# Stores of second-level block sums moved behind the loads on SyncE's queue, in the MLP of a one-core transformer layer

## The chip, the cores and the metric

The kernel runs on one core of a Trainium2 chip. The metric is device time in microseconds (us) of one execution, as the median of several runs. A profile of one execution says what each engine did and when: TensorE (PE, with weight loads as PEld), VectorE (DVE), ScalarE (ACT), GpSimd (POOL) and SyncE (SP, which here only issues transfers).

## The reference

One layer of a hybrid encoder on 1024 tokens of width 1024, in float32: two attention groups side by side, a cross-attention into 256 memory tokens, and a squared-ReLU MLP with hidden width 4096. Each is wrapped in root-mean-square norms and added to the residual. The change lies in the MLP alone:

```python
h = rmsnorm(x, g_ff_pre[l])
y = jnp.square(jax.nn.relu(h @ w_ff1[l])) @ w_ff2[l]
x = x + rmsnorm(y, g_ff_post[l])
```

## The kernel before

Every float32 operand of a product is split in a high and a low part, and a product is three matmuls (lines 193, 194, 195: high by high, low by high, high by low). The MLP's two matrix products are done by a seven-product block scheme: sums of blocks are multiplied instead of the blocks themselves, and the results are recombined.

The first half of the MLP is a loop over `j` = 0 to 15 (`NP` = 16), and the order of its instructions on each engine is the order in which the code is written. Iteration `j` works on two of the 32 row blocks of `w_ff1`, called blocks `j` and `j + 16`. What an iteration does, in this order:

- GpSimd makes the weight sums of iteration `j + 1` from its two raw blocks (`nxt.sums`, lines 2080 to 2082, and `nxt.sum4`, line 2087). They go into the tiles `sc` and `sd`.
- SyncE issues the load of the first raw block of iteration `j + 2` (`after.load(0)`, line 1833, tile `wf`).
- TensorE multiplies into the PSUM banks `px`, `pz`, `px` again (accumulating), `pv` and `pz` again (accumulating), 12 matmuls each. In the iterations below `AHEAD` = 7 the first row of products was done earlier and stored; it is loaded back a step ahead (`reload`, line 2102, tile `p1r`, two halves `p1` and `g11`). From `j` = 7 on it is multiplied in place.
- VectorE adds the products up. Line 2261 makes `u2` from the first `px` and `p1`; only after it may TensorE accumulate into that bank. Then `sums` of the iteration before (lines 2316, 2318, 2320 and 2322) is run, the low part of the next weights is made (`v0lo_s` or `v1lo_s`, line 1848), and lines 2277 and 2281 make `u3` and `g22` from the second `px` and from `pz`; only after line 2281 may TensorE accumulate into `pz`. Next come `wlo_s1a`, line 2299, the low part of `sd` (`u0lo_s` or `u1lo_s`) and line 2305.
- ScalarE makes the high parts of the weights and squares the clipped results (`relu2`, lines 1865 and 1866).
- SyncE stores the results: `put` (line 1869) into the buffers `gd`, and `put_parts` (lines 1885, 1887) into `gi1` and `gi5`. The loads of the second raw block of iteration `j + 2` (`after.load(1)`) and of `p1r` are issued in mid iteration, after line 2281.

Two of the seven results are taken through the block scheme a second time. For these the sums of two neighbouring iterations (an even and an odd `j`) are formed by `put_sums` in the even iteration that follows: four VectorE operations of 128x256 (lines 1893 to 1896) for form 1 in mid iteration, and four for form 5 at its end. `put_sums` returns a function that issues two stores (lines 1898 and 1899: `s12` and `s34` to `gi1S` or `gi5S`). These are the second-level forms:

```python
        return lambda: (
            nc.sync.dma_start(gi[n, ("S1", "S2")][s][:, :, k, :], s12.rearrange("p (a n) -> p a n", a=2)),
            nc.sync.dma_start(gi[n, ("S3", "S4")][s][:, :, k, :], s34.rearrange("p (a n) -> p a n", a=2)))
```

SyncE issues transfers strictly in the order written. It waits before each until its data are there or its target is free, and what stands behind waits with it. Raw blocks rotate through three buffers, and the tiles of results and sums through 18.

Of the kernel before, what the change touches and what calls it, by code (L numbers as in the profile page):

```python
# [135 lines left out]
def build(ctx, tc, nc, out, t):  # L136
# [13 lines left out]
    def mm_tile(shape, name, tag="mm"):  # L150
        return psp.tile(shape, F32, tag=tag, bufs=2, name=name)

    def u4(name, shape, dt=F32R):

        return up.tile(list(shape), dt, tag="u4", bufs=30, name=name)
# [1649 lines left out]
    def t2(name):  # L1805
        if region[0]:
            return pr.tile([P, HT], F32, tag="t2", bufs=9, name=name)
        return pf.tile([P, HT], F32, tag="t2", bufs=18, name=name)
# [3 lines left out]
    def bank(name, tag=None):  # L1812
        if tag is None:
            tag = ("mm", "s", "tr", "pv")[banks[0] % 4]
            banks[0] += 1
        return mm_tile([P, HT], name, tag)
# [47 lines left out]
    def relu2(c):  # L1864
        nc.scalar.activation(c, c, AF.Relu)
        nc.scalar.activation(c, c, AF.Square)
# [22 lines left out]
    def put_sums(n, j, c):  # L1889

        k, s, e = j // 2 % 4, j // 8, even.pop(n)
        s12, s34 = t2(f"s12_{n}{j}"), t2(f"s34_{n}{j}")
        nc.vector.tensor_add(s12[:, :HQ], e[:, HQ:], c[:, HQ:])
        nc.vector.tensor_sub(s12[:, HQ:], s12[:, :HQ], e[:, :HQ])
        nc.vector.tensor_sub(s34[:, :HQ], e[:, :HQ], e[:, HQ:])
        nc.vector.tensor_sub(s34[:, HQ:], c[:, :HQ], s12[:, HQ:])
# [3 lines that stand above are left out]
# [200 lines left out]
    def reload(j):  # L2100
        both = u4(f"p1r{j}", (P, 2, HT), F32)
        nc.sync.dma_start(both, p1d[j])
        saved[j] = both[:, 0, :], both[:, 1, :]
# [54 lines left out]
    def raw_b(q, k):  # L2158
        r = u4(f"wg{q}_{k}_{len(rows_b)}", (P, D), F32)
        nc.sync.dma_start(r, t["w_ff2"][q, k])  # L2160
        return r

    def fetch(s):

        n, k = steps[s]
        ra = wp.tile([P, D], F32, tag="wraw", bufs=3, name=f"ra{s}")
        rows_a[s] = ra
        if n in (("i", 0), ("i", 1)):
            name, h = inner[k // 2], k % 2
            nc.sync.dma_start(ra, gi[(1, 5)[n[1]], name][h].rearrange("p a b -> p (a b)"))  # L2170
            quads = {"A11": (0, 1), "A12": (2,), "S2": (3,), "S1": (), "S3": (0,), "S4": (3,), "A22": (2,)}[name]
            rows_b[s] = []
            for q in quads:
                rows_b[s].append(u4(f"wi{q}_{s}", (P, D), F32))
                nc.sync.dma_start(rows_b[s][-1], t["w_ff2q"][n[1], q, h])
            return
        i, name = order[n]
        nc.sync.dma_start(ra, gd[i][k].rearrange("p a b -> p (a b)"))
        if name == "T1":
            rows_b[s] = (raw_b(W12, k), raw_b(W11, k))  # L2180
        else:
            rows_b[s] = (raw_b({"B11": W11, "T2": W22, "T3": W11, "T4": W21}[name], k),)
# [50 lines left out]
        ops[s] = (ah, al, bh, bl)  # L2233

    with manual:
        sums = lambda: []
        for j in range(NP):
            more = j + 1 < NP
            after = Weights(j + 2) if j + 2 < NP else None
            w = cur.w  # L2240
            if more:
                nxt.sums()
                nxt.sum4()
            if after:
                after.load(0)
            elif more:
                fetch(0)
            if j < AHEAD:
                p1, g11 = saved.pop(j)
                x = bank(f"px{j}")  # L2250
            else:
                x, _, g11, add = first_row(j, w["a"])
                add()
            if not more:
                fetch(1)
                fetch(2)
                prepare(0)
            product(x, w["s23"], 0, XT["T2"], more=j >= AHEAD)
            u2 = t2(f"u2_{j}")
            if j < AHEAD:  # L2260
                nc.vector.tensor_add(u2, x, p1)
            else:
                nc.scalar.activation(u2, x, AF.Copy)
            forms = sums()
            relu2(g11)
            put(j, 0, g11)
            z = bank(f"pz{j}")
            product(z, w["s1a"], 0, XT["T1"])
            if more:
                if j + 1 >= AHEAD:  # L2270
                    nxt.split("a")
                if j:
                    nxt.split("s23")
            product(x, w["s23"], HT, XT["T3"], more=True)
            u3 = t2(f"u3_{j}")
            if j < AHEAD:
                nc.vector.tensor_add(u3, x, p1)
            else:
                nc.scalar.activation(u3, x, AF.Copy)
            g22 = t2(f"g22_{j}")  # L2280
            nc.vector.tensor_add(g22, z, u3)
            for form in forms[:1]:
                form()
            if more and not j:
                nxt.split("s23")
            if after:
                after.load(1)
            elif not more:
                prepare(1)
                fetch(3)  # L2290
            if j + 1 < AHEAD:
                reload(j + 1)
            v = bank(f"pv{j}")
            product(v, w["s1a"], HT, XT["T4"])
            if more:
                nxt.split("s1a")
            relu2(g22)
            put(j, 2, g22)
            nc.vector.tensor_sub(u3, u3, v)
            product(z, w["s4"], 0, XT["B22"], more=True)  # L2300
            if more:
                nxt.split("s4")
            relu2(u3)
            put_parts(1, j, u3)
            nc.vector.tensor_add(u2, z, u2)
            for form in forms[1:]:
                form()

            if not more:
                relu2(u2)  # L2310

            def sums(j=j, u2=u2, u3=u3, g11=g11, g22=g22):
                if j + 1 < NP:
                    relu2(u2)
                s1, s2, s4g = t2(f"s1_{j}"), t2(f"s2_{j}"), t2(f"s4_{j}")
                nc.vector.tensor_add(s1, u2, g22)
                put(j, 3, s1)
                nc.vector.tensor_sub(u2, g11, u2)
                put(j, 5, u2)
                nc.vector.tensor_sub(s2, s1, g11)  # L2320
                put(j, 4, s2)
                nc.vector.tensor_sub(s4g, u3, s2)
                put_parts(5, j, s4g)
                return [lambda: put_sums(1, j, u3)(), lambda: put_sums(5, j, s4g)()] if j % 2 else []

            cur, nxt = nxt, after
        prepare(2)
# [141 lines left out]
        for s, (n, k) in enumerate(steps[:-3]):  # L2469
            if s and s < len(steps) - 2:  # L2470
                prepare(s + 2)
            for read in reads:
                read()
            del reads[:]
            if s == 1:
                forms = sums()
            if s in (2, 3):
                forms.pop()()
            if s == 4:
                pfs.close()  # L2480
            if s + 4 == len(steps):
                prepare(s + 3)
            if s + 4 < len(steps):
                fetch(s + 4)
            if isinstance(n, tuple):
                inner_multiply(s)
                if k % 2:
                    reads.append(lambda x=n[1], p=k // 2: inner_read(x, p))
                for call in later[:1]:
                    call()  # L2490
                del later[:1]
                continue
            if k == 0:
                if n == 0:
                    X = four(f"fx{n}", ("mm", "s"))
                elif n == 3:
                    Y = four(f"fy{n}", ("tr", "pv"))
            banks = Y if n == 3 else X
            multiply(banks, range(4), [s], n in (2, 4, 6))
            for call in later[:1 if n < 6 else 2]:  # L2500
                call()
            del later[:1 if n < 6 else 2]
            if n == 6 and k in (3, 4):
                residual(2 * k - 2)
                residual(2 * k - 1)
            if k == NK - 1:
                for tp in range(4):
                    gather(n, tp, banks[tp])
                finished(n)
# [75 lines left out]
```

## Time and profile before

| | |
|---|---|
| median of 3 runs | 1463.97 us (1461.88 to 1464.31) |
| profiled execution | 1463.95 us, its span 1462.1 us |
| mean granted TensorE clock | 0.998 |
| TensorE busy | 1445.3 us, 99% of the span |
| VectorE, ScalarE, GpSimd busy | 1074.2, 844.6, 418.9 us |
| transferred | 255.29 MB, 175 GB/s in the mean |
| loop over `j`, iterations 2 to 5 | about 905 to 971 us of the span |

A row of a timeline holds the start, the duration, the engine, the line, the operation, and output and inputs by tile name (buffer numbers left out); in brackets stands how long the engine had been idle and what ended that. SPq rows are the issuing of a transfer, not the transfer. Matmuls overlap: the next starts before the one before it is shown as ended.

### The profile page before, as it was taken

The page shows a single profiled execution, that of the slowest core. Times are in us where ns is not written, and L with a number is a line of the kernel's source. Part 1 is how long each engine was busy: PE and PEld are TensorE (multiplying, and loading weights), DVE is VectorE, ACT ScalarE, POOL GpSimd, SP SyncE. Part 2 cuts the span into 40 slices and gives each one's busy share as a digit, 9 for nine tenths or more (in the row PEclk, how much of TensorE's full clock was granted, in tenths as well). Part 3 has the DMA queues.
Part 4 walks back from the last instruction along what each step waited for, and adds up shares of the span by engine and source line. Part 5 has one row for each costly group of instructions (what it writes and reads, how often), then busy time and mean ns, then how long its engine had stood idle before and what let it go on. Part 6 is the DMA issues. An engine that isn't in the chain of part 4 may idle for free.

```text
span 1462.1 us, 21876 instructions
## 1 busy us (share of the span) xinstructions
PE 1445.3 (99%) x7553; PEld 1232.0 (84%) x7553; DVE 1074.2 (73%) x1830; ACT 844.6 (58%) x1465; POOL 418.9 (29%) x520
## 2 busy tenths in 40 slices
PE   8999999999999999999999999999999999999998
PEld 8988888888889888888788888778888888888886
DVE  6777777767668847976873787785555776789897
ACT  6567677767677836555653455455555545555553
POOL 1245456545455301421321414333232000000003
PEclk9999999999999999999999999999999999999999
DMA  7132324321315595542531637775556897786885
GB/s 275 48 94 73 83 65 142 85 82 46 94 58 165 169 318 173 186 174 88 187 130 44 205 127 252 245 230 175 166 178 203 298 345 255 244 283 231 279 285 203
DMA packets 104351, 255.29 MB, mean 175 GB/s; under 512 B 11673, under 2 KB 30113, under 8 KB 104241
## 3 DMA queue, kind: packets, MB, share of 16 engines
q1 hardware_dynamic: 104096, 253.65, 52.6%
q8 instruction: 59, 0.97, 0.3%
q14 instruction: 52, 0.42, 0.1%
q10 hardware_dynamic: 144, 0.26, 0.1%
HBM read 184.07 MB, written 61.40 MB: 168 GB/s over the span
## 4 chain that ended last, share of the span: by engine, by line
PE 90%; DMA 3%; DVE 3%; issue 1%; ACT 1%; POOL 1%; SPq 0%; DVEq 0%; ACTq 0%
PE pv L754 4%; PE fx L194 4%; PE fx L193 4%; PE fx L195 4%; PE ptr L711 4%; PE px L194 3%; PE px L195 3%; PE px L193 3%; PE k L193 2%; PE q L193 2%; PE q L195 2%; PE q L194 2%; PE k L195 2%; PE k L194 2%; PE v L195 2%; PE v L193 2%
## 5 line engine op out<-in xcount | busy, mean ns | idle before, releaser
L717 DVE TENSOR_TENSOR phl<-ptr,phl 128x512 fp32r<-128x512 f32 (+1 forms) x152 | 92.5, 616 | 31.6 <-ACT phl L720 30.6
L720 ACT ACTIVATE phl<-ptr 128x512 fp32r<-128x512 f32 (+1 forms) x152 | 79.6, 539 | 40.3 <-PE ptr L711 38.5
L2357 POOL TENSOR_SCALAR rf<-sf 128x1 f32<-128x1 f32 x7 | 7.0, 1004 | 315.6 <-ACT jf L2338 315.4
L2229 ACT ACTIVATE whif<-ra 128x1024 fp32r<-128x1024 f32 x45 | 47.6, 1058 | 76.8 <-PE fx L194 34.7
L754 PE MATMUL pv<-phl,vs 128*128 128x512 f32 (+1 forms) x304 | 85.2, 366 | 0.2 <-DVE phl L717 0.2
L2231 DVE TENSOR_TENSOR wlof<-ra,whif 128x1024 fp32r<-128x1024 f32 x45 | 55.0, 1222 | 35.9 <-ACT whif L2229 35.8
L193 PE MATMUL fx<-vhif,whif 128*128 128x512 f32 x168 | 65.6, 391 | 0.0
L194 PE MATMUL fx<-vlof,whif 128*128 128x512 f32 x168 | 65.6, 391 | 0.0
L195 PE MATMUL fx<-vhif,wlof 128*128 128x512 f32 x168 | 65.4, 389 | 0.0
L754 PEld LDWEIGHTS pv<-phl,vs 128*128 128x128 f32 x304 | 55.2, 188 | 11.0 <-DVE phl L717 0.8
L2080 POOL TENSOR_TENSOR sc<-wf,wf 128x512 f32<-128x512 f32 x14 | 20.1, 1434 | 150.6 <-DMA wf<-in_w_ff 148.8
L768 POOL TENSOR_TENSOR o<-o 64x256 f32<-64x256 f32 x64 | 47.8, 747 | 52.7 <-DVE o L766 34.3
L766 DVE TENSOR_TENSOR o<-pv,o 64x512 f32<-64x512 f32 x64 | 44.0, 687 | 13.6 <-ACT o L771 12.2
L193 PE MATMUL k<-hT_hi,whik 128*128 128x512 f32 x128 | 53.6, 419 | 0.0
L193 PE MATMUL q<-hT_hi,whiq 128*128 128x512 f32 x128 | 51.6, 403 | 0.0
L193 PE MATMUL mq<-h2T_hi,whimq 128*128 128x512 f32 x128 | 51.4, 402 | 0.0
L195 PE MATMUL k<-hT_hi,wlok 128*128 128x512 f32 x128 | 50.4, 393 | 0.0
L193 PE MATMUL yw<-whiwo,yT_hi 128*128 128x512 f32 x128 | 50.3, 393 | 0.1
L195 PE MATMUL mq<-h2T_hi,wlomq 128*128 128x512 f32 x128 | 50.2, 392 | 0.2 <-DVE wlomq L455 0.2
L194 PE MATMUL k<-hT_lo,whik 128*128 128x512 f32 x128 | 50.3, 393 | 0.0
L195 PE MATMUL q<-hT_hi,wloq 128*128 128x512 f32 x128 | 50.2, 392 | 0.0
L194 PE MATMUL mq<-h2T_lo,whimq 128*128 128x512 f32 x128 | 50.2, 392 | 0.1
(715 smaller groups left out, 5214.6 us busy)
## 6 DMA issues: line engine op xcount, KB each, us to landing
wg<-in_w_ff SPq DMA_DIRECT2D x48, 512.0 KB, 6.2
ra<-gd SPq DMA_DIRECT2D x40, 512.0 KB, 4.4
wf<-in_w_ff SPq DMA_DIRECT2D x38, 512.0 KB, 4.5
wi<-in_w_ff2q SPq DMA_DIRECT2D x28, 512.0 KB, 5.5
wrawmq<-in_w_mq SPq DMA_DIRECT2D x16, 512.0 KB, 4.2
gd<-s SPq DMA_DIRECT2D x32, 256.0 KB, 2.1
gd<-g SPq DMA_DIRECT2D x25, 256.0 KB, 3.2
wrawq<-in_w_qk SPq DMA_DIRECT2D x8, 512.0 KB, 4.5
```

The costliest lines, as they stand in the source:

```text
L193: nc.tensor.matmul(ps, lh, rh, start=start, stop=False, skip_group_check=more)
L194: nc.tensor.matmul(ps, lh, rl, start=False, stop=False, skip_group_check=more)
L195: nc.tensor.matmul(ps, ll, rh, start=False, stop=stop, skip_group_check=more)
L711: nc.tensor.transpose(tr[:, m, :], sp[:, k * P:(k + 1) * P], ident)
L717: flow.put("V", at, 0.7, lambda: nc.vector.tensor_sub(pl[:, live, :], tr[:, live, :], f(ph[:, live, :])), done)
L720: flow.put("S", flow.end, 0.6, lambda ph=ph, tr=tr, live=live: nc.scalar.activation(ph[:, live, :], tr[:, live, :], AF.Copy), split)
L754: nc.tensor.matmul(pv[:, :, qs_, :], v, hl[:, :, hs, :], start=c == 0 and turn == 0, stop=last)
L766: flow.put("V", at, 0.7, lambda: nc.vector.tensor_add(o2[own], pv[own, :, :, ::step], o2[own]), lambda end: (free["pv"].give(end), flow.pu ...
L768: free["pv"].give(end), flow.put("G", end, 0.8, lambda: nc.gpsimd.tensor_add(o2[own, 0], o2[own, 0], o2[own, 1]), store)))
L2080: eng.tensor_sub(sc[:, k1], r0[:, k0], r1[:, k0])
L2229: nc.scalar.activation(ah, ra, AF.Copy)
L2231: nc.vector.tensor_sub(al, ra, f(ah))
```

## The change

The stores of a second-level form are no longer issued by the code that computes its sums. `put_sums` is called at the same place as before, so the four additions stay where they are, but the function that it returns is kept in a list `stores` and called later: for form 1 after the load of the second raw block and of `p1r`, for form 5 after the load of the first raw block at the head of the next iteration. In the second half of the MLP, where the last pair's forms are made, the two steps are still done at once.

```diff
-        sums = lambda: []
+        sums, stores = (lambda: []), []
         for j in range(NP):
...
             if after:
                 after.load(0)
             elif more:
                 fetch(0)
+            for store in stores:
+                store()
             if j < AHEAD:
                 p1, g11 = saved.pop(j)
                 x = bank(f"px{j}")
...
             nc.vector.tensor_add(g22, z, u3)
-            for form in forms[:1]:
-                form()
+            stores = [form() for form in forms[:1]]
             if more and not j:
                 nxt.split("s23")
             if after:
                 after.load(1)
...
             if j + 1 < AHEAD:
                 reload(j + 1)
+            for store in stores:
+                store()
             v = bank(f"pv{j}")
             product(v, w["s1a"], HT, XT["T4"])
...
             nc.vector.tensor_add(u2, z, u2)
-            for form in forms[1:]:
-                form()
+            stores = [form() for form in forms[1:]]
...
-                return [lambda: put_sums(1, j, u3)(), lambda: put_sums(5, j, s4g)()] if j % 2 else []
+                return [lambda: put_sums(1, j, u3), lambda: put_sums(5, j, s4g)] if j % 2 else []
...
-                forms.pop()()
+                forms.pop()()()
```

On TensorE, VectorE, ScalarE and GpSimd the order of instructions is the same before and after. On SyncE, iteration `j` = 2 and the head of `j` = 3 read as follows (the first `wf` with its `p1r` is for `j` = 4 and 3, the second `wf`, behind `gi1A`, for `j` = 5; `s_11` and `s_51` are the sums of forms 1 and 5):

```order
 L1869 DMA gd_1_9277<-p1r_10155 128x512
+L1833 DMA wf_10276<-in_w_ff 128x1024
+L2102 DMA p1r_10278<-p1d_9335 128x1024
 L1898 DMA gi1S_9346<-s_11_10270 256x1x256
 L1899 DMA gi1S_9348<-s_11_10271 256x1x256
-L1833 DMA wf_10278<-in_w_ff 128x1024
-L2102 DMA p1r_10280<-p1d_9335 128x1024
 L1869 DMA gd_1_9293<-g_2_10268 128x512
 L1885 DMA gi1A_9342<-u_2_10266 128x256
+L1833 DMA wf_10335<-in_w_ff 128x1024
 L1898 DMA gi5S_9354<-s_51_10323 256x1x256
 L1899 DMA gi5S_9356<-s_51_10324 256x1x256
-L1833 DMA wf_10337<-in_w_ff 128x1024
```

Two loads moved ahead of form 1's pair of stores and one ahead of form 5's; the stores keep their order among themselves. The same happens around `j` = 4 and 5.

From `j` = 7 on there is no `p1r` to load back. On SyncE, iteration `j` = 8 and the head of `j` = 9 (the first `wf` is for `j` = 10, the second for `j` = 11):

```order
+L1833 DMA wf_11092<-in_w_ff 128x1024
 L1898 DMA gi1S_9346<-s_17_11086 256x1x256
 L1899 DMA gi1S_9348<-s_17_11087 256x1x256
-L1833 DMA wf_11094<-in_w_ff 128x1024
 L1869 DMA gd_4_9296<-g_8_11084 128x512
 L1885 DMA gi1A_9343<-u_8_11082 128x256
+L1833 DMA wf_11149<-in_w_ff 128x1024
 L1898 DMA gi5S_9354<-s_57_11137 256x1x256
 L1899 DMA gi5S_9356<-s_57_11138 256x1x256
-L1833 DMA wf_11151<-in_w_ff 128x1024
```

One load moved ahead of each pair of stores. The even iterations 6, 10 and 12 read alike; at `j` = 14 there is no load left to pass, and nothing moved.

## The prediction

> **What bounds the kernel now.** The share of busy time by engine comes first, then the stages around the edit, then who keeps TensorE waiting there.
>
> ```profile
> PE 1445.3 (99%) x7553; PEld 1232.0 (84%) x7553; DVE 1074.2 (73%) x1830; ACT 844.6 (58%) x1465; POOL 418.9 (29%) x520
> 885.00:980.00 95.00, 90.64 (x390) 73.66 (x389) 69.90 (x94) 46.49 (x68) 39.21 (x28) 0.98 0.72 244
> 980.00:1140.00 160.00, 160.00 (x707) 132.27 (x706) 95.23 (x143) 84.00 (x126) 43.73 (x32) 1.00 0.55 179
> 1140.00:1200.00 60.00, 60.00 (x266) 49.59 (x265) 44.14 (x50) 30.10 (x38) 0.00 (x0) 1.00 0.93 335
> PE pz L193 <- DVE g L2281: 4.0, 2, 2.2
> ```
>
> In the stage rows the columns after the length are busy PE, PEld, DVE, ACT, POOL, then granted clock and DMA share. TensorE is full nearly everywhere, so only its holes can be won. The edit acts in iterations j = 2 to 13, and of that stretch only 885 to 980 us has holes: 4.4 us idle, plus a clock of 0.98. The last row names the holes: two waits of the product L193 for the addition L2281 on VectorE. The two later stage rows are full (160.00 of 160.00, 60.00 of 60.00), so what is won ahead of them is not taken back by a wait that exists today.
>
> The matmuls show both places, j = 3 and j = 5.
>
> ```profile
> 925.90 0.39 PE L193 MATMUL pz<-T_hi,whi_s1a 128*128 128x512 f32 x1
> 928.39 0.39 PE L195 MATMUL pz<-T_hi,wlo_s1a 128*128 128x512 f32 x1
> 936.70 0.47 PE L193 MATMUL pz<-B_hi,u1hi_s 128*128 128x512 f32 x1 [2.19 <-DVE g L2281]
> 940.65 0.39 PE L194 MATMUL pz<-B_lo,u1hi_s 128*128 128x512 f32 x1
> 941.10 0.39 PE L193 MATMUL px<-T_hi,v0hi_s 128*128 128x512 f32 x1
> 936.70:940.80 4.10, 4.10 (x11) 3.25 (x12) 2.27 (x3) 2.85 (x5) 1.22 (x1) 0.58 0.85 300
> 957.42 0.39 PE L193 MATMUL pz<-T_hi,whi_s1a 128*128 128x512 f32 x1
> 968.26 0.47 PE L193 MATMUL pz<-B_hi,u1hi_s 128*128 128x512 f32 x1 [1.85 <-DVE g L2281]
> 968.57 0.40 PE L194 MATMUL pz<-B_lo,u1hi_s 128*128 128x512 f32 x1
> ```
>
> From 925.90 to 928.39 there are 11 steps, 0.2265 us each. From the first product pz of an iteration to the next iteration's px stand 48 matmuls, 48 x 0.2265 = 10.87 us without a hole. In j = 3 it took 941.10 - 925.90 = 15.20, an excess of 4.33. Of that 1.68 is no wait: after the 2.19 us hole the clock is 0.58, and ten matmuls take 940.65 - 936.70 = 3.95 instead of 2.27. In j = 5 the same stretch ends at 968.57 + 11 x 0.2265 = 971.06, so it took 13.64, an excess of 2.77; the clock held. **The most that can be won is 4.33 + 2.77 = 7.1 us.**
>
> Why L2281 is late: the chain that ended last, the store queue, and the engines it feeds.
>
> ```profile
> 922.09 3.46 DMA p1r<-p1d
> 926.14 5.44 DMA wf<-in_w_ff
> 916.87 0.56 SPq L1869 DMA_DIRECT2D gd<-p1r  x1
> 920.18 0.52 SPq L1898 DMA_DIRECT2D gi1S<-s  x1
> 921.46 0.58 SPq L1833 DMA_DIRECT2D wf<-in_w_ff  x1
> 922.09 0.44 SPq L2102 DMA_DIRECT2D p1r<-p1d  x1
> 912.32 1.29 POOL L2087 TENSOR_TENSOR sd<-wf,sc 128x512 f32<-128x512 f32 x1
> 926.75 1.29 POOL L2080 TENSOR_TENSOR sc<-wf,wf 128x512 f32<-128x512 f32 x1 [13.14 <-DMA wf<-in_w_ff]
> 928.12 1.29 POOL L2081 TENSOR_TENSOR wf<-wf 128x512 f32<-128x512 f32 x1
> 931.18 1.63 POOL L2087 TENSOR_TENSOR sd<-wf,sc 128x512 f32<-128x512 f32 x1
> 927.93 0.63 ACT L1865 ACTIVATE p1r<-p1r 128x512 f32<-128x512 f32 x1 [2.54 <-DMA p1r<-p1d]
> 922.47 0.69 DVE L1848 TENSOR_TENSOR u1lo_s<-sd,u1hi_s 128x512 fp32r<-128x512 f32 x1
> 923.99 0.42 DVE L1893 TENSOR_TENSOR s<-s,s 128x256 f32<-128x256 f32 x1
> 927.99 0.69 DVE L2261 TENSOR_TENSOR u<-px,p1r 128x512 f32<-128x512 f32 x1 [2.46 <-issue]
> 928.60 1.36 DVE L2316 TENSOR_TENSOR s<-u,g 128x512 f32<-128x512 f32 x1
> 931.58 1.78 DVE L2320 TENSOR_TENSOR s<-s,p1r 128x512 f32<-128x512 f32 x1
> 934.01 1.22 DVE L1848 TENSOR_TENSOR v0lo_s<-sc,v0hi_s 128x1024 fp32r<-128x1024 f32 x1
> 935.86 0.69 DVE L2281 TENSOR_TENSOR g<-pz,u 128x512 f32<-128x512 f32 x1
> ```
>
> SyncE waits from 917.43 to 920.18 for the forms' sums, and the loads `wf` and `p1r` stand behind that store. `p1r` lands at 927.9; only then can L2261 run (its product px had ended when pz began, 925.90). From 927.99 VectorE is busy without a gap until L2281 ends at 936.55: a chain of 8.56 us, where TensorE has 36 matmuls, 8.16 us, and reaches that point at 934.3. The chain is that long because GpSimd's weight sums, released by `wf`, run at the same time: L2316 and L2320 take 1.36 and 1.78 where such an operation takes 0.69 (u1lo_s, same size).
>
> **The change part by part.**
>
> *The loads.* No computing instruction is added, dropped or moved; in j = 2, 4, ... 12 the mid-iteration loads pass form 1's two stores, and the load at the next head passes form 5's two. The buffer of `wf` in j = 2 was last read by GpSimd's L2087, 912.32 + 1.29 = 913.61, so the load can be issued when the store before it is, at 917.43 + 0.1 = 917.5, and `p1r` at 918.1. Both are 4.0 us earlier. At the next head, `wf` for j = 5 moves from 926.14 to about 924.3; nobody waits for it yet.
>
> *The stores.* They still wait for the same sums, so gi1S goes out at 920.2 as before. The forms' stores are read only in the second half of the MLP, and their tiles are two of 18 buffers; a delay under 1 us is free. Queued behind them is only what was behind them before. This costs 0.
>
> *`p1r` in j = 3.* Issued 4.0 earlier it lands at about 923.9, before px ends. L2261 is no longer held by it, and could start at 926.1: 1.9 us of the chain are gone.
>
> *`wf` in j = 3, and the contention that moves with it.* From issue to GpSimd's start:
>
> ```profile
> 952.98 0.57 SPq L1833 DMA_DIRECT2D wf<-in_w_ff  x1
> 958.32 1.28 POOL L2080 TENSOR_TENSOR sc<-wf,wf 128x512 f32<-128x512 f32 x1 [13.35 <-DMA wf<-in_w_ff]
> 966.59 0.40 SPq L1833 DMA_DIRECT2D wf<-in_w_ff  x1
> 970.55 1.30 POOL L2080 TENSOR_TENSOR sc<-wf,wf 128x512 f32<-128x512 f32 x1 [6.17 <-DMA wf<-in_w_ff]
> ```
>
> 5.3 us (here and in j = 2) and 4.0 us at the quickest: GpSimd starts between 921.5 and 922.8; I take 922.5, 5.0 after the issue. Its four operations then lie over VectorE's u1lo_s and the four operations of the second form (from 923.99) instead of over L2316 to L2320. How that goes the rows show: GpSimd's L2081 ends at 928.12 + 1.29 = 929.41, and L2316, begun within it, ends at 929.96, 0.55 later; L2087 ends at 932.81, L2320 at 933.36, again 0.55. An operation that reads SBUF twice does its work only after GpSimd's current one; L2261, with one operand in PSUM, took its 0.69 under GpSimd. The form's operations are 128x256 (0.42 against 0.69, a row not seen under GpSimd here), so their bounds are 0.42, unhindered, and a full hand-over, 0.42 - 0.69 + 0.55 = 0.28 after each end of GpSimd, whose next operation ends about 1.15 later (929.96 to 931.10, the start of L2087 at 931.18 less 0.08).
>
> The Trainium skill, "SBUF — State Buffer", section "SBUF: two separate sides", calls this an exclusive lock between GpSimd and a VectorE operation with two SBUF inputs: whichever starts first holds the pair for the whole instruction. It speaks against the change, since it predicts the full hand-over for the form's operations too; by it alone the sum below would be 1458.9, by free running 1456.9. The trace agrees with it for 128x512.
>
> With the full hand-over and a start at 922.5: u1lo_s ends 923.16, GpSimd's first 924.3; first form operation 924.6, GpSimd 925.75; second 926.05, 927.2; third 927.5, 928.65; fourth 928.95; then L2261 until 929.6. TensorE's second product px, which accumulates on the bank that L2261 reads, is due at 928.62 and starts about 1.0 late. From there GpSimd is done: L2316 to the end of L2281 take 4 x 0.66 + 1.22 + 2 x 0.7 = 5.3, ending at 934.9, and TensorE needs it 24 matmuls, 5.44 us, after px starts, at 935.1. So there is no second hole, and a hole of 1.0 us is well below 1.85, after which the clock held. With a start at 921.5 one form operation less collides, L2261 ends at 929.0 and the hole is 0.4. I take 0.9 per iteration, near the slower end since two of three intervals were 5.3.
>
> *j = 5* is the same, with `wf` issued up to 0.6 later for the reason next: 0.9 as well.
>
> *j = 4 and 6, unchanged code, but later against TensorE.* VectorE's chain now stands nearer behind TensorE, so the loads issued after L2322 do too.
>
> ```profile
> 935.02 0.40 SPq L1833 DMA_DIRECT2D wf<-in_w_ff  x1
> 939.58 1.28 POOL L2080 TENSOR_TENSOR sc<-wf,wf 128x512 f32<-128x512 f32 x1 [6.76 <-DMA wf<-in_w_ff]
> ```
>
> Today GpSimd starts 1.5 us before px of j = 4 (941.10). After: L2322, the last ahead of v0lo_s, ends about 932.3 instead of 934.0; the load follows it by 1.0 as today, at 933.3; GpSimd starts 4.56 later as today, at 937.9; and px of j = 4 is at 941.10 - (4.33 - 0.9) = 937.7. GpSimd starts with px instead of 1.5 before it, and two of VectorE's sums collide with it, at about 1.0 each (1.78 - 0.69 and less). Unhindered the chain is 0.7 for L2261 and the 5.3 from above, with the collisions 8.0, and 8.16 is allowed. I count 0.
>
> *j = 7 to 13.* `p1r` is gone there. The sums collide with forms as above, up to 4 us of VectorE, and what hides it is VectorE's idle time behind the forms:
>
> ```profile
> 1028.67 0.69 DVE L1910 TENSOR_TENSOR g<-py,p 128x512 f32<-128x512 f32 x1 [2.86 <-issue]
> 1033.15 0.69 DVE L2316 TENSOR_TENSOR s<-u,g 128x512 f32<-128x512 f32 x1 [3.78 <-ACT u L1866]
> ```
>
> 2.86 + 3.78 us per iteration; without that cover it would be a hole of about 1 us in each of four. I count 0, neither gain nor loss.
>
> *The sum.* 7.1 - 2 x 0.9 = 5.3 us. The profiled execution took 1463.95 us (span 1462.1 and 1.85 around it), the median of the runs is 1463.97, so the two agree: 1463.95 - 5.3 = **1458.7 us**. One run took 1461.88, 2.1 less, which a run without the stretch of slow clock (1.68) would nearly explain.
>
> The Trainium skill, "TensorE: Matmul & The Clock Gate", section "Part 1: The HAM clock gate", says that the clock halves after an idle window of about 3.4 us that runs freely; the trace partly agrees: 2.19 us sufficed once, 1.85 did not. By that page the 1.68 is a matter of where the window fell, and 5.3 would be 3.6 in an execution that had no slow stretch.
>
> **The rivals.** Differences under 0.2%, 2.9 us, are within what a measurement of this kernel can tell from none.
>
> *The hole moves to L2261* (0.12). If `wf` lands later than I take, 6.5 us after its issue since stores and `p1r` share the engines, GpSimd starts at 924.0, the four form operations all collide, L2261 ends at 930.65, px is 2.0 late, and the second hole is about the old one less 0.6. For it: DMA is busy 0.72 in this stage. Against it: no interval here was over 5.4. Gain 2 x 0.6, with the slow clock kept: 1462.8.
>
> *Slower: the collision passes to j = 4 and 6* (0.08). If GpSimd starts over 1.5 us after px there, its sums cover L2316 to L2320 as they do today in j = 3 (926.75 against px's end at 925.90), and TensorE waits there instead, each time with the slow clock: 2 x 4.33 = 8.7 lost, 5.3 won, 1467.3. Against it: the load would have to slip by another 1.5 us.
>
> *The change does nothing* (0.08): the loads are issued earlier but land as late, because the DMA engines are full with the stores issued up to 916.87. Then 1463.95. Against it: transfers issued 3 us later land within 5.3.
>
> **How the numbers follow.** The forecast, 0.72: 1456.9 (no hole left) to 1460.5 (holes of 1.8). The range reaches up into the first rival, to 1462.0, leaving out about half of that one and the two others, some 0.2. Faster than 1461.0: the forecast, 0.72, and a quarter of the first rival, 0.75. Slower than 1466.9: 0.08. Within: 0.17.
>
> **What would show it.** Right: in j = 2 and 4 `wf` and `p1r` issued 2.5 us or more ahead of gi1S; the row of L193 waiting for L2281 gone or under 0.5 in total; a wait of px for L2261 of 0.4 to 1.0, twice; the clock 1.00 from 885 to 980; form 5's operations L1893 to L1896 stretched at the end of even j. Wrong: those four at 0.42 with GpSimd's sums beside them; a wait for L2281 in j = 4 or 6; `wf` still landing 9 us after 917.5; new holes after 980 us.

## The result, and the profile after

The changed kernel takes 1458.65 us (median of 5 runs) against 1463.97 us for the kernel before (5 runs beside it). The ratio is 0.9966, with a 95% interval of 0.9952 to 0.9979. The medians differ by 5.3 us, which is the gain that was forecast; by the interval it lies between 3.1 and 7.0 us. The profiled execution took 1457.34 us, its span 1455.5.

The profile of the changed kernel: busy time by engine, the same stages as in the prediction (length, then busy PE, PEld, DVE, ACT, POOL, granted clock, DMA share), and all waits of TensorE from 890 to 1200 us.

```profile
PE 1443.5 (99%) x7553; PEld 1231.0 (85%) x7553; DVE 1089.6 (75%) x1830; ACT 844.4 (58%) x1465; POOL 423.3 (29%) x520
885.00:980.00 95.00, 93.61 (x411) 76.57 (x410) 77.42 (x101) 50.22 (x74) 41.78 (x30) 1.00 0.77 256
980.00:1140.00 160.00, 160.00 (x708) 132.48 (x707) 105.60 (x137) 83.42 (x125) 44.24 (x31) 1.00 0.54 179
PE px L193 <- DVE u L2263: 1.3, 2, 0.8
```

The two waits of pz for g (4.0 us) are gone. In their place stand two waits of px for u, 1.3 us together. The clock of the stage is 1.00 where it was 0.98, and the stage behind is as full as before. VectorE is busy for 15 us more (1089.6 against 1074.2) and the kernel is faster all the same: an operation that stands still beside GpSimd counts as busy (u1lo_s below is shown with 1.52 us, 0.69 before).

The timeline of the changed kernel in j = 2 and 3, by engine: SyncE's issues, GpSimd's weight sums, VectorE, TensorE. Lines behind the edit have moved by a few numbers; L2263 and L2283 are what L2261 and L2281 were.

```profile
916.10 0.40 SPq L1833 DMA_DIRECT2D wf<-in_w_ff  x1
916.55 0.44 SPq L2102 DMA_DIRECT2D p1r<-p1d  x1
918.73 0.52 SPq L1898 DMA_DIRECT2D gi1S<-s  x1
922.90 0.37 SPq L1833 DMA_DIRECT2D wf<-in_w_ff  x1
925.44 0.53 SPq L1898 DMA_DIRECT2D gi5S<-s  x1
920.70 1.29 POOL L2080 TENSOR_TENSOR sc<-wf,wf 128x512 f32<-128x512 f32 x1 [8.51 <-DMA wf<-in_w_ff]
922.07 1.62 POOL L2081 TENSOR_TENSOR wf<-wf 128x512 f32<-128x512 f32 x1
923.77 1.36 POOL L2082 TENSOR_TENSOR sc<-wf,wf 128x512 f32<-128x512 f32 x1
925.21 1.36 POOL L2087 TENSOR_TENSOR sd<-wf,sc 128x512 f32<-128x512 f32 x1
935.94 1.30 POOL L2080 TENSOR_TENSOR sc<-wf,wf 128x512 f32<-128x512 f32 x1 [9.37 <-DMA wf<-in_w_ff]
921.02 1.52 DVE L1848 TENSOR_TENSOR u1lo_s<-sd,u1hi_s 128x512 fp32r<-128x512 f32 x1
923.06 0.91 DVE L1893 TENSOR_TENSOR s<-s,s 128x256 f32<-128x256 f32 x1
924.01 1.40 DVE L1894 TENSOR_TENSOR s<-s,s 128x256 f32<-128x256 f32 x1
925.34 1.52 DVE L1895 TENSOR_TENSOR s<-s 128x256 f32<-128x256 f32 x1
926.78 0.41 DVE L1896 TENSOR_TENSOR s<-s,s 128x256 f32<-128x256 f32 x1
927.12 0.68 DVE L2263 TENSOR_TENSOR u<-px,p1r 128x512 f32<-128x512 f32 x1
924.46 0.39 PE L193 MATMUL pz<-T_hi,whi_s1a 128*128 128x512 f32 x1
927.85 0.50 PE L193 MATMUL px<-T_hi,v1hi_s 128*128 128x512 f32 x1 [0.51 <-DVE u L2263]
936.14 0.39 PE L193 MATMUL px<-T_hi,v0hi_s 128*128 128x512 f32 x1
956.18 0.50 PE L193 MATMUL px<-T_hi,v1hi_s 128*128 128x512 f32 x1 [0.84 <-DVE u L2263]
```

The loads now go out 2.6 us ahead of form 1's first store (916.10 against 918.73), where they followed it. GpSimd is done at 926.57, so the chain from u to g behind it runs without collisions. The profiled execution gained more than the medians, 6.6 us: pz of j = 3 begins at 924.46 instead of 925.90, 1.44 us earlier, ahead of anything that the edit touches. The remaining 5.1 to 5.2 us are won behind it.

For all comparisons below I use one measure. The **excess** of an iteration is the time from its first px to the first px of the next one, less its 60 matmuls at 0.2266 us each. It holds waits and slow clock together. In the changed kernel j = 3 has 0.80 us and j = 5 has 1.14.

### The profile page after: what moved, and what is told of

Read it like the earlier page. It is cut to its first block, busy times and chain, and to the rows that moved or that the text cites. A ratio compares the mean times of both kernels' runs of the same rounds, so it can differ in the third digit from the quotient of the medians.

```text
span 1455.5 us, 21885 instructions
## 1 busy us (share of the span) xinstructions
PE 1443.5 (99%) x7553; PEld 1231.0 (85%) x7553; DVE 1089.6 (75%) x1830; ACT 844.4 (58%) x1465; POOL 423.3 (29%) x520
## 4 chain that ended last, share of the span: by engine, by line
PE 94%; DVE 3%; issue 1%; ACT 1%; DMA 0%; SPq 0%; DVEq 0%; ACTq 0%
PE pv L754 4%; PE fx L193 4%; PE fx L194 4%; PE fx L195 4%; PE ptr L711 4%; PE px L193 3%; PE px L194 3%; PE px L195 3%; PE k L193 2%; PE yw L193 2%; PE mq L195 2%; PE q L193 2%; PE q L194 2%; PE q L195 2%; PE k L194 2%; PE mq L194 2%
## 5 line engine op out<-in xcount | busy, mean ns | idle before, releaser
L194 PE MATMUL q<-hT_lo,whiq 128*128 128x512 f32 x128 | 50.2, 392 | 0.0
```

Of the source, the lines that this page charges most:

```text
L194: nc.tensor.matmul(ps, lh, rl, start=False, stop=False, skip_group_check=more)
```

## The experiments

The theory, as in the prediction: the loads of `wf` and `p1r` behind form 1's stores make the hole; both are won by passing these stores; what is left is the hand-over between GpSimd's sums and VectorE's; form 5's part of the edit is worth nothing. The rivals: form 5's part matters; one of the loads would have been enough; the rest has another cause.

The runs in one table. The gain is one minus the ratio, times 1463; the excess is that of the profiled execution, in us. The experiments were run in groups, each beside its own runs of the kernel before (medians of 1463.34, 1462.99 and 1462.77 us), so kernels of different groups are compared by their ratios. The edits of the experiments are against the changed kernel, unless another is named.

| kernel | ratio to before, 95% interval | gain, us | j=3 | j=4 | j=5 | j=6 | sum |
|---|---|---|---|---|---|---|---|
| before | | | 4.32 | 0 | 2.77 | 0.23 | 7.3 |
| the change | 0.9966 [0.9952, 0.9979] | 5.0 | 0.80 | 0 | 1.14 | 0.30 | 2.2 |
| only form 1 passed | 0.9988 [0.9979, 0.9998] | 1.8 | 1.02 | 0.45 | 1.90 | 5.50 | 9.3 with 0.4 in j=7 |
| only form 5 passed | 0.9999 [0.9990, 1.0007] | 0.1 | 3.04 | 0 | 3.14 | 1.26 | 7.4 |
| only `p1r` ahead | 0.9977 [0.9967, 0.9986] | 3.4 | 1.55 | 0 | 1.87 | 0.25 | 3.7 |
| only `wf` ahead | 0.9987 [0.9978, 0.9996] | 1.9 | 0.49 | 1.25 | 1.68 | 2.56 | 6.0 |
| `p1r` ahead, form 5 passed | 0.9977 [0.9969, 0.9986] | 3.4 | 1.56 | 0 | 1.95 | 0.19 | 3.7 |
| loads behind g22's store | 1.0000 [0.9991, 1.0010] | 0 | 3.0 | 0 | 3.3 | 0.19 | 6.5 |
| form 5's sums later | 0.9965 [0.9952, 0.9977] | 5.1 | 0 | 0 | 0 | 0.27 | 0.3 |

The ratio stands for all executions of a kernel, the excess for the profiled one alone, and they need not agree. With only form 1 passed the profiled execution took 1464.01 us, 2.2 more than the median of that kernel, so its excess of 9.3 us, more than before the change, is larger than in a usual execution. With only `wf` ahead it took 1463.04 us against a median of 1462.36.

**Only form 1's stores are passed.** Form 5's pair goes out as before the change, ahead of the next head's load:

```
             nc.vector.tensor_add(u2, z, u2)
-            stores = [form() for form in forms[1:]]
+            for form in forms[1:]:
+                form()()
+            stores = []
```

> Only the stores of form 1 are moved (mid-iteration loads ahead of them); those of form 5 stay ahead of the load at the next head. Theory (the mid-iteration loads of p1r and wf are what was late): the whole gain, 1458.7 us, within 0.7 of the change; no wait of L193 for L2281; waits of px for L2261 of 1.3 us in all as in the change. Rival (the load at the head matters too): part of the gain is missing, 1460.5 or more, and a wait that the change does not show.

It took 1461.79 us against 1463.34, about a third of the gain. My expectation failed and the rival was right. Waits of TensorE, then SyncE, ScalarE, GpSimd and TensorE in the timeline, then two stretches in the stage view, all of this kernel:

```profile
PE pz L193 <- DVE g L2283: 3.0, 2, 2.8
PE px L193 <- DVE u L2263: 2.3, 2, 1.6
925.46 0.52 SPq L1898 DMA_DIRECT2D gi5S<-s  x1
927.80 0.60 SPq L1833 DMA_DIRECT2D wf<-in_w_ff  x1
961.51 0.40 SPq L1833 DMA_DIRECT2D wf<-in_w_ff  x1
961.96 0.52 SPq L2102 DMA_DIRECT2D p1r<-p1d  x1
969.56 0.63 ACT L1865 ACTIVATE p1r<-p1r 128x512 f32<-128x512 f32 x1 [1.63 <-DMA p1r<-p1d]
968.47 1.29 POOL L2080 TENSOR_TENSOR sc<-wf,wf 128x512 f32<-128x512 f32 x1 [11.99 <-DMA wf<-in_w_ff]
979.55 0.76 PE L193 MATMUL pz<-B_hi,u0hi_s 128*128 128x512 f32 x1 [2.81 <-DVE g L2283]
961.00:969.00 8.00, 8.00 (x37) 6.64 (x36) 4.55 (x7) 4.23 (x7) 0.53 (x1) 1.00 1.03 364
979.00:983.00 4.00, 3.44 (x8) 2.80 (x9) 3.97 (x8) 2.15 (x4) 1.80 (x1) 0.50 0.72 249
```

The changed kernel, in the stretch in which its `wf` of that iteration is on the way (issued at 959.73, GpSimd's start at 964.21):

```profile
959.00:964.00 5.00, 5.00 (x23) 4.13 (x23) 4.63 (x6) 2.66 (x5) 0.00 (x0) 1.00 0.91 322
```

The early `wf` puts GpSimd's sums over form 5's, so form 5's store is ready late (925.46), and the head's load behind it leaves at 927.80, not at 922.90 as in the change. The same happens in j = 5 (957.35 against 951.01). The mid-iteration loads follow it 4.2 us later, 8.7 in the change. While they travel the DMA engines are full (a busy share of 1.03 from 961 to 969 us; 0.91 in the change while its `wf` travels). `wf` takes 6.96 us from issue to GpSimd's start, 4.48 in the change, and `p1r` 7.6 us to its first use, and now both are waited for. GpSimd's sums fall on the three additions behind u in j = 6 (1.42, 1.67 and 1.78 us where each takes 0.69 alone), TensorE waits 2.8 us, and the clock is 0.50 behind it. Of the 5.50 us of j = 6, 2.5 are this slow clock. This is the rival "the collision passes to j = 4 and 6" of the prediction. What kept it out of the change is the very part of the edit that I had counted at nothing.

**Only form 5's stores are passed.** The other half:

```
             nc.vector.tensor_add(g22, z, u3)
-            stores = [form() for form in forms[:1]]
+            for form in forms[:1]:
+                form()()
+            stores = []
```

> Only the stores of form 5 are moved (the load at the next head ahead of them); form 1's stay ahead of the mid-iteration loads. Theory: nothing is gained, 1463.9 us as before, and L193 waits for L2281 about 4 us in two places as before. Rival (the head's load matters): 1 us or more faster than before and a shorter wait for L2281.

1463.11 us against 1463.34, no difference. Alone it does nothing; the two halves together give 5.0 us where alone they give 1.8 and 0.1.

**Only `p1r` is ahead of form 1's stores**, in the even iterations; `wf` stays behind them, and form 5 goes as before:

```
+            if stores and j + 1 < AHEAD:
+                reload(j + 1)
+            for store in stores:
+                store()
             if after:
                 after.load(1)
...
-            if j + 1 < AHEAD:
+            if not stores and j + 1 < AHEAD:
                 reload(j + 1)
-            for store in stores:
-                store()
```

> Of the mid-iteration loads only p1r is ahead of form 1's stores; wf stays behind them, and form 5's stores stay where they were. Theory (two separate delays of one VectorE chain, either of which is enough to undo most of the hole): L2261 starts when px has ended instead of 1.9 us later, GpSimd's weight sums start as late as before and still stretch L2316 to L2320, so the chain of 8.56 us against TensorE's 8.16 leaves a hole of 0.4 to 0.8 us per odd iteration at pz, none at px: excess 0.6 to 1.0 twice, 1458.0 us (1457.5 to 1459.5), form 5's four operations at 0.42. Rival 1 (wf alone matters): about 1463, holes of 2 us at pz. Rival 2 (p1r alone matters): as the theory, so that the next run decides.

1460.23 us against 1463.34: 3.1 us by the medians, 3.4 by the ratio, less than I expected. Of this kernel, TensorE's wait, then GpSimd, VectorE and TensorE in j = 3:

```profile
PE pz L193 <- DVE g L2283: 2.9, 2, 1.6
924.89 1.29 POOL L2080 TENSOR_TENSOR sc<-wf,wf 128x512 f32<-128x512 f32 x1 [12.28 <-DMA wf<-in_w_ff]
925.02 0.69 DVE L2263 TENSOR_TENSOR u<-px,p1r 128x512 f32<-128x512 f32 x1 [0.57 <-PE px L195]
934.44 0.47 PE L193 MATMUL pz<-B_hi,u1hi_s 128*128 128x512 f32 x1 [1.30 <-DVE g L2283]
```

u no longer waits for `p1r`: it follows its product. But GpSimd starts with it and lies over the whole chain, which takes 9.3 us from 925.02 to the end of g (934.29), longer than the 8.56 before. The early `p1r` alone shortens the hole from 2.19 to 1.30; it does not close it. By the times alone this kernel can't be told from the change: its gain lies between 2.0 and 4.8 us, that of the change between 3.1 and 7.0. The difference rests on the profiles, 3.7 us of excess against 2.2.

**Only `wf` is ahead**, with `p1r` behind form 1's stores and form 5 as before:

```
-            if j + 1 < AHEAD:
-                reload(j + 1)
             for store in stores:
                 store()
+            if j + 1 < AHEAD:
+                reload(j + 1)
```

> Of the mid-iteration loads only wf is ahead of form 1's stores; p1r stays behind them, issued 0.6 us earlier than before, and form 5's stores stay where they were. Theory (either delay alone is enough): GpSimd starts 4 us earlier and stretches form 5's operations instead of L2316 to L2320; L2261 starts at about the time that p1r lands, which is also when the stretched operations end, so that this is as good as the change: 1458.9 us (1457.5 to 1460.3), a wait of px for L2261 of 0.3 to 0.9 twice, no wait at pz. Rival 2 (p1r alone matters, as the chain of waits names it): L2261 held as before and holes at pz of over 1.5 us, 1462 or more.

1462.36 us against 1463.34, 1.0 us by the medians and 1.9 by the ratio, where I expected nearly all of the gain. The place itself comes out well: j = 3 has 0.49 us left. What is lost is elsewhere, 1.25 in j = 4 and 2.56 in j = 6, with the same late head load as above (928.72 us). So both experiments in which `wf` is early and form 5's stores stay ahead of the head's load lose in the same two iterations.

**`p1r` ahead and form 5 passed**, to see whether form 5's part has a worth of its own, or only beside an early `wf`. It is the kernel with `p1r` ahead, with form 5's line as in the change.

> p1r alone ahead of form 1's stores, wf behind them, and form 5's stores moved as in the change. Theory, new (form 5's move pays only because its sums are stretched once wf is early, so that its stores would hold the head's load): here wf is late, the sums are not stretched, and form 5's move is worth nothing: 1460.2 us as with p1r alone, within 0.7, waits at pz of about 2.9 us in all. Rival (an earlier load at the head is worth something by itself): 1 us or more faster than p1r alone, 1459 or less.

1459.57 us against 1462.99, the ratio 0.9977 as without form 5's part, and TensorE's wait for g is 3.0 us where it was 2.9. With `wf` late the part is worth nothing. It pays only where the early `wf` has stretched form 5's sums.

**The loads are put behind one store more.** The kernel before, with the loads of even iterations moved the other way, behind the store of g22:

```
-            if after:
-                after.load(1)
...
-            if j + 1 < AHEAD:
-                reload(j + 1)
+            if j % 2 or not j:
+                if after:
+                    after.load(1)
+                if j + 1 < AHEAD:
+                    reload(j + 1)
...
             put(j, 2, g22)
+            if j and j % 2 == 0:
+                if after:
+                    after.load(1)
+                if j + 1 < AHEAD:
+                    reload(j + 1)
```

> The order of before, with the mid-iteration loads of even j moved one store further back, behind that of g22, 1.6 us later. Theory (the holes follow the issue of these loads): excess in j = 3 and 5 grows by up to 1.6 each, with the slow clock perhaps in both: 1466 us (1465 to 1469). Rival (the loads' landing is set by the traffic, not by the issue): as before, 1463.3.

1463.16 us against 1462.99: no slower. SyncE, GpSimd and VectorE of this kernel:

```profile
921.35 0.37 SPq L1833 DMA_DIRECT2D wf<-in_w_ff  x1
926.22 1.28 POOL L2080 TENSOR_TENSOR sc<-wf,wf 128x512 f32<-128x512 f32 x1 [13.39 <-DMA wf<-in_w_ff]
927.45 0.69 DVE L2261 TENSOR_TENSOR u<-px,p1r 128x512 f32<-128x512 f32 x1 [2.72 <-issue]
```

My expectation of 1466 us failed, and the time is that of the rival. But the dose was smaller than the 1.6 us that I had reckoned with. The store of g22 was ready when its turn came, so `wf` left 1.31 us after form 1's second store instead of 0.61, and GpSimd started 4.87 us after the issue, not 5.3. Of the further 0.7 us in the queue 0.4 disappears in how the transfers land. So small a delay does not decide between the theory and the rival.

**The kernel before once more**, for the stretch of slow clock.

> The kernel before once more, for a second profile. Theory: waits for L2281 in j = 3 and 5 again, about 4 us; the slow clock after a hole of 2.2 us is a matter of chance, present in slow executions (1464 and up) and absent in quick ones (1462).

It took 1461.81 us. Its stage from 885 to 980 us, and the first matmul behind its hole in j = 3:

```profile
885.00:980.00 95.00, 90.01 (x393) 73.06 (x392) 72.11 (x95) 47.10 (x69) 38.33 (x28) 1.00 0.72 242
935.57 0.47 PE L193 MATMUL pz<-B_hi,u1hi_s 128*128 128x512 f32 x1 [2.21 <-DVE g L2281]
```

The hole is the same, 2.21 us against 2.19, and the clock stays at 1.00. Two more profiles have the same hole in j = 3, that with only form 5 passed (2.16 us) and that with the loads behind g22's store (2.18), and both have a clock of 1.00 behind it. So the slow clock came in one of four. The excess of this second profile is 2.94 in j = 3 and 3.16 in j = 5, 6.4 in all with j = 6, against the 7.3 of the first profile.

**Form 5's sums are computed later**, in the next iteration behind g, where GpSimd is idle, and stored behind the loads there. The rest of the change stays:

```
-    def put_sums(n, j, c):
+    def put_sums(n, j, c, e=None):
...
-        k, s, e = j // 2 % 4, j // 8, even.pop(n)
+        k, s, e = j // 2 % 4, j // 8, even.pop(n) if e is None else e
...
-            stores = [form() for form in forms[:1]]
+            stores = [form() for form in forms[:1]] + [form(e) for form, e in late]
...
-            stores = [form() for form in forms[1:]]
+            late = [(form, even.pop(5)) for form in forms[1:]]
+            stores = []
```

> On top of the change, form 5's four sums are computed in the next iteration, behind L2283 (L2281 of before), and its stores follow that iteration's mid loads. Theory (what is left of the holes is GpSimd's weight sums stretching form 5's operations ahead of L2263, L2261 of before): nothing stands between L2308 and L2263, the waits of px for L2263 (1.3 us) are gone, excess in j = 3 and 5 under 0.2 each, and 1.9 us less than the change: 1456.8 us (1456.0 to 1457.6). Rival (the rest comes from p1r or wf landing late): the same holes of px as in the change, 1458.7.

1456.97 us against 1462.99, ratio 0.9965. In the profile the excess is gone in j = 3, 4 and 5: what was left in the change was the hand-over. Whether this version beats the change was asked again, both beside the same runs of the kernel before.

> The changed kernel once more, unchanged, so that it and the version with form 5's sums moved to the next iteration share a chip and the runs of the kernel before. Both theories: ratio to the kernel before 0.9955 to 0.998, a hole of 0.5 to 0.9 us in front of the x matmuls in j = 3 and in j = 5.

> The version with form 5's sums computed behind g of the next iteration, once more, beside the changed kernel on the same chip. If the rest of the excess in j = 3 and j = 5 (0.80 and 1.14 us in the changed kernel's profile) is the hand-over between the GpSimd sums and form 5's VectorE sums, this one is faster than the changed kernel by 1.5 to 2.2 us in the median, with no wait of TensorE in the j loop. If something else comes late in its place, the two are within 0.7 us.

The change took 1457.54 us and this version 1457.93; both have the ratio 0.9965 to the kernel before (0.9953 to 0.9977, and 0.9952 to 0.9978). It does not beat the change, although its loop is better. First the change in this pair (two stages, the first px of j = 1, an issue of the second half's weights `wg` on SyncE, two operations on VectorE that wait for such loads):

```profile
885.00:980.00 95.00, 93.70 (x411) 76.67 (x410) 77.49 (x101) 50.25 (x74) 40.99 (x30) 1.00 0.76 255
1140.00:1300.00 160.00, 160.00 (x864) 139.19 (x864) 120.94 (x122) 83.83 (x98) 0.00 (x0) 1.00 0.83 291
894.46 0.39 PE L193 MATMUL px<-T_hi,v1hi_s 128*128 128x512 f32 x1
1163.13 0.87 SPq L2160 DMA_DIRECT2D wg<-in_w_ff  x2
1169.41 1.23 DVE L2206 TENSOR_TENSOR wg<-wg,wg 128x1024 f32<-128x1024 f32 x1 [2.64 <-DMA wg<-in_w_ff]
1183.46 1.23 DVE L2206 TENSOR_TENSOR wg<-wg,wg 128x1024 f32<-128x1024 f32 x1 [4.19 <-DMA wg<-in_w_ff]
```

Then the same lines of the version with form 5's sums later, and the matmul that waits:

```profile
885.00:980.00 95.00, 95.00 (x420) 78.47 (x419) 77.18 (x103) 50.35 (x74) 43.62 (x31) 1.00 0.77 260
1140.00:1300.00 160.00, 159.08 (x857) 137.53 (x856) 120.94 (x124) 82.08 (x96) 0.00 (x0) 1.00 0.81 282
895.78 0.39 PE L193 MATMUL px<-T_hi,v1hi_s 128*128 128x512 f32 x1
1163.75 0.87 SPq L2160 DMA_DIRECT2D wg<-in_w_ff  x2
1171.28 1.22 DVE L2206 TENSOR_TENSOR wg<-wg,wg 128x1024 f32<-128x1024 f32 x1 [3.60 <-DMA wg<-in_w_ff]
1185.08 1.23 DVE L2206 TENSOR_TENSOR wg<-wg,wg 128x1024 f32<-128x1024 f32 x1 [3.52 <-DMA wg<-in_w_ff]
1188.72 0.50 PE L194 MATMUL fy<-bl,ah 128*128 128x512 f32 x1 [0.76 <-DVE bl L2232]
```

Counted from the first px of j = 1, TensorE ends the loop 2.1 us earlier (the excess of the change in this pair is 2.16, of this version 0). The load of `wg` is issued only 0.7 us earlier (267.97 against 268.67), and the first operation on `wg` shown starts 0.55 us later (275.50 against 274.95). The second one, 0.3 us later (289.30 against 289.00), again follows a wait for its load, and it leads to the low part `bl` that TensorE then waits for. So TensorE runs into products fy whose weights are not ready, and the steps between matmuls there are 1.7 us longer in all than in the change. The first profile of this version shows the same (2.3 us), the first of the change 0.1. The gain of the loop is given back at the start of the second half. Why the loads of `wg` did not come forward with the loop was not tried.

## Why the prediction was right, and where it was not

- **The ceiling of 7.1 us.** The profile before has 4.32 and 2.77 us by the measure above, so the size is right for that execution. But the repeated profile of before has 2.94 and 3.16, without slow clock, and of four profiles with that hole only the first has the 1.68 us of it. What can be won in a usual run is nearer 6.1. The change takes 7.3 - 2.2 = 5.1 us of excess off the first profile and 6.4 - 2.2 = 4.2 off the second, so some luck is in how closely the sum of 5.3 was met. The Trainium skill, "TensorE: Matmul & The Clock Gate", section "Part 1: The HAM clock gate", has the clock fall by where a free-running idle window lies; two equal holes with different clocks agree with that, while the page's window of about 3.4 us is longer than the 2.2 us that sufficed once.
- **The issues.** Right in j = 2, not quite in j = 4: predicted for both was 2.5 us or more ahead of form 1's store, measured are 2.6 and 2.0 (`wf` at 944.87, the store at 946.86). Form 1's own store in j = 2 goes out at the predicted time (918.73, which is 920.17 with the 1.44 us of the earlier start).
- **GpSimd's start.** Predicted 922.5, in the same count 922.1, 4.6 us after the issue.
- **The hand-over on form 5's operations.** Right in its full form, with one operation of the form less than in the main case of the prediction: u1lo_s collides too (1.52 us), and the fourth of the form no longer does. Those of 128x256 take 0.91, 1.40 and 1.52 us where the fourth, alone, takes 0.41, and the first three end 0.28 us after the end of a GpSimd operation (923.97 against 923.69; 925.41 against 925.13; 926.86 against 926.57), the 0.28 that the prediction worked out. The Trainium skill, "SBUF — State Buffer", section "SBUF: two separate sides", gives the exclusive lock; for this shape too the trace now agrees with it.
- **The residual of 0.9 us in each of j = 3 and 5.** Measured 0.80 and 1.14, as waits of px for u of 0.51 and 0.84, within the 0.4 to 1.0 named. The version with form 5's sums moved away has neither, so the cause holds.
- **j = 4 and 6 at nothing.** Measured 0 and 0.30 (0.23 before). GpSimd starts at 935.94, 0.2 us before px, where I had put it 0.2 us behind.
- **j = 7 to 13 at nothing.** Measured nothing.
- **Wrong: "At the next head, `wf` for j=5 moves from 926.14 to about 924.3; nobody waits for it yet."** The time is right (922.90, which is 924.34 in the same count). The worth is not. I compared the load with its place before the change, and not with the place it would have had once the first half of the edit stretched form 5's sums: 927.80 in the first experiment, 4.9 us later than in the change. With that, 3.2 us of the 5.0 hang on it. The sum came out because the change holds both parts.
- **Wrong by its place: the rival in which "the collision passes to j = 4 and 6".** It was held off by "the load would have to slip by another 1.5 us". In the experiments with an early `wf` and form 5's stores ahead it did slip so far (with form 1 alone, GpSimd starts 2.8 us after px of j = 6, 968.47 against 965.71), and j = 6 loses 5.5 and 2.6 us. In the change it does not occur.

Not settled: how much of the gain `p1r` brings beside an early `wf`. The kernel with only `wf` ahead kept form 5's stores in front of the head's load and lost in j = 4 and 6, as the kernel with only form 1 passed did, while its j = 3 has even less excess than the change (0.49 against 0.80). An early `wf` with form 5 passed and `p1r` left behind was not run; it may be worth as much as the change. Also not settled: that the late head load and the mid loads slow each other down is read from the busy share (1.03 against 0.91) and the landing times; no run changed the traffic alone.

## What to carry to other kernels

A store that waits for a result holds every load behind it in its queue, so price a reordering by which loads pass which waiting store, and by what reaches other engines earlier as a consequence. Two halves of an edit can be worth 1.8 and 0.1 us apart and 5 together: when one half makes an operation slower, look again at what its late result now holds up, instead of pricing the other half against the old trace. When a loop is full, look at the first load of the next stage before spending more on the loop.

## What the runs showed of the hardware that was not expected

- A hole of 2.2 us on TensorE was followed by about half clock in one profile (0.58) and by full clock in three others (1.00); behind 2.8 us it was 0.50.
- GpSimd is held up too: its operation of 1.29 us takes 1.62 beside VectorE's sums (L2081 at 922.07). The collision is paid for on both engines.
- A load of `wf` took 4.5 us from issue to GpSimd's start at a DMA share of 0.91 and 7.0 us at 1.03; an issue 0.7 us later (the loads behind one store more) did not show in the time of the kernel.
